# A decoder layer's MLP: the second matrix product done as seven block products instead of eight

## The chip, the cores and the metric

The kernel runs on one core of a Trainium2 chip as a single program. The metric is device time in microseconds (us). Three runs of the kernel before gave 1417.79, 1421.07 and 1423.99 us; the median, 1421.07 us, is the time to compare with. The execution that the profile shows is a fourth one.

## The reference, cut to what matters

One layer handles 1024 prompt tokens and 8 sample tokens together, so the activations have 1032 columns. The part that matters here is its end, the squared-ReLU MLP with 1024 channels and 4096 hidden units, and the final norm:

```python
hf = _rmsnorm(x, norm_ffn_g)
a = jax.nn.relu(jnp.einsum('btd,df->btf', hf, w_up))
x = x + jnp.einsum('btf,fd->btd', a * a, w_down)
...
y_prompt = _rmsnorm(xp, norm_final_g)
y_sample = _rmsnorm(xs, norm_final_g)
```

All numbers are float32. Ahead of the MLP stand a pooling mixer, gated linear attention and a cross-attention into 256 memory tokens.

## The kernel before

Activations lie transposed: 128 channels on the partitions, the 1032 tokens along the free dimension. TensorE multiplies in a rounded float32 format, so each operand is split into a high and a low part: ScalarE casts the value (`hi`, line 155), VectorE subtracts the cast from the value (`lo`, line 156), and a product is three matmuls, hi by hi, hi by lo and lo by hi. The helper `split` does that for weights and activations alike.

The MLP's way up (lines 1027 to 1160) already uses Winograd's form of Strassen's algorithm. `w_up` is cut into 2 by 2 quarters (halves of the input channels, halves of the hidden units), the activations into 2 by 2 quarters (halves of the channels, and tokens 0 to 511 against 512 to 1031), and seven products of sums of quarters, named "1" to "7", take the place of eight. A product of a 512-token block is one matmul of 512 columns per weight block and part; one of 520 tokens is two of 260 columns. `first_products` does products "1" and "2" for each of 16 blocks m of 128 hidden units and leaves quarter c11 in DRAM; `other_products` then does the other five for each m, adds them up on VectorE, applies ReLU and square on ScalarE (lines 1088, 1089) and writes the three quarters c22, c21 (`u3`) and c12 to the scratch tensor `hd` in DRAM from ScalarE's queue (line 1090).

The way down (lines 1163 to 1326) is a plain product. It walks over eight blocks `fb` of 512 hidden units: four tiles of hidden activations are loaded from `hd` and split (`block`), and for each of the 8 output chunks c of 128 channels a weight tile is loaded and split (`down_w`), 4 x 3 x 3 matmuls of 344 columns accumulate in PSUM (`gemm_steps`, line 192), and VectorE adds the result to the residual X (line 1207). The last block is walked in three column groups of 384, 384 and 264 tokens (line 1239) so that the final norm of finished tokens (`finish`) can run beside it; the last three token tiles are normed at the end.

All DMA transfers on the way down are issued by SyncE (SP), in its program order. The order in which instructions stand on each engine is made by the framework's scheduler from the code's order and the pools. Tiles come from pools with a fixed number of buffers: `S` has 19 large slots; `tmp` has 4 (line 68); `wp` holds raw and split weights (line 67); `mp` and `accp` are PSUM.

Of the kernel before, what the change touches and what calls it, by code (L numbers as in the profile page):

```python
# [8 lines left out]
F32 = mybir.dt.float32  # L9
# [7 lines left out]
P = 128  # L17
D = 1024
# [42 lines left out]
def body(ctx, tc, a, o):  # L61
# [968 lines left out]
    hd = dr.tile([2 * MU, P, NT], F32, name="hd")  # L1030
# [56 lines left out]
    def hidden_out(c, half, t):  # L1087
        A.activation(out=t, in_=t, func=AF.Relu)
        A.activation(out=t, in_=t, func=AF.Square)
        A.dma_start(hd[c][:, TH[half]], t)  # L1090

    def first_products(m):
# [8 lines left out]
        hidden_out(m, 0, c11)  # L1101

    def other_products(m):
# [36 lines left out]
        hidden_out(MU + m, 1, c22)  # L1140
        hidden_out(MU + m, 0, u3[:, :HA])
        hidden_out(m, 1, c12)
# [20 lines left out]
    X = []  # L1163
    for i in range(4):
        t = slot([P, 2, NT], F32, "x%d" % i)
        SY.dma_start(t, xd[2 * i:2 * i + 2].rearrange("c p n -> p c n"))
        X.append(t)

    gfin = slot([P, 2, 512], F32, "gfin")
    SY.dma_start(gfin.rearrange("p x n -> p (x n)"), a["norm_final_g"].unsqueeze(0).broadcast_to([P, D]))  # L1170
    WD = []

    w_down = a["w_down"][0].rearrange("(i k p) c -> p i k c", i=2, p=P)

    def down_raw(fb, c, name):

        raw = wp.tile([P, FC, P], F32, tag="raw", name=name, bufs=3)
        for i in range(2):
            SY.dma_start(raw[:, 2 * i:2 * i + 2, :], w_down[:, i, 2 * fb:2 * fb + 2, c * P:(c + 1) * P])
        return raw  # L1180

    def down_w(fb, c):
        return w_split(down_raw(fb, c, "wdn"))

    def block(fb, k):

        t = T("hid")
        SY.dma_start(t, hd[(k // 2) * MU + 2 * fb + k % 2])
        b_ = slot([P, 2, NT], F32R, "b")
        split(b_[:, 0, :], b_[:, 1, :], t)  # L1190
        return two(b_)

    def last_w(c):

        wd = slot([P, 2, 2, FC, P], F32R, "wd")
        for i in range(2):
            raw = down_raw(FB - 1, c + i, "wdl")
            split(wd[:, i, 0], wd[:, i, 1], raw)
            WD.append(wd[:, i])

    B = [block(0, k) for k in range(FC)]
    for fb in range(FB - 1):
        nxt = []
        for c in range(KC):
            acc = gemm_chunk(down_w(fb, c), B, "wdn")
            xc = X[c // 2][:, c % 2, :]
            V.tensor_tensor(out=g3(xc), in0=acc, in1=g3(xc), op=ALU.add)  # L1207
            if c % 2:
                nxt.append(block(fb + 1, c // 2))
                if fb == FB - 2:  # L1210
                    last_w(c - 1)
        B = nxt


    def turn_out(pt, t, c):

        n = min(P, NT - t * P)
        PE.transpose(pt[:n, (c % 4) * P:(c % 4 + 1) * P], X[c // 2][:, c % 2, t * P:t * P + n], ident)

    def rows(t):  # L1220
        return o["y_p"][0, t * P:(t + 1) * P, :].rearrange("p (x n) -> p x n", x=2)

    def finish(t):
        pt = accp.tile([P, NG, 512], F32, tag="acc", name="pty")
        for c in range(KC):
            turn_out(pt[:, c // 4], t, c)
        y = T("y", D).rearrange("p (x n) -> p x n", x=2)
        sc = sm.tile([P, 4], F32, tag="fin", name="sc")
        A.activation(out=y, in_=pt[:, :2], func=AF.Square, accum_out=sc[:, 0:1])
        V.tensor_scalar(out=sc[:, 1:2], in0=sc[:, 0:1], scalar1=1.0 / D, scalar2=EPS, op0=ALU.mult, op1=ALU.add)  # L1230
        rsqrt_(sc[:, 2:3], sc[:, 1:2], sc[:, 3:4])
        V.scalar_tensor_tensor(out=y, in0=pt[:, :2], scalar=sc[:, 2:3], in1=gfin, op0=ALU.mult, op1=ALU.mult)
        SY.dma_start(rows(t), y)

    def down(c, t0, ks, acc):
        q0, q1 = t0 * P, min((t0 + 3) * P, NT)
        for k in ks:
            for i, (x, y) in enumerate(((0, 0), (0, 1), (1, 0))):
                PE.matmul(acc[:, :q1 - q0], WD[c][:, x, k, :], B[k][y][:, q0:q1],  # L1239
                          start=(k == 0 and i == 0), stop=(k == FC - 1 and i == 2))  # L1240
        if ks[-1] == FC - 1:
            xc = X[c // 2][:, c % 2, q0:q1]
            V.tensor_tensor(out=xc, in0=acc[:, :q1 - q0], in1=xc, op=ALU.add)

    def acc_l():
        return mp.tile([P, 512], F32, tag="m", name="accl")


    wide = accp.tile([P, NG, 512], F32, tag="acc", name="accw")
    acc = [acc_l(), acc_l(), wide[:, 0], wide[:, 1]]  # L1250
    for ks in (range(FC - 1), range(FC - 1, FC)):
        for c in range(4):
            down(c, 0, ks, acc[c])
    for c in range(4, KC):
        down(c, 0, range(FC), acc_l())

    for c in range(KC):
        down(c, 3, range(FC), acc_l())
        if c < 3:
            finish(c)  # L1260
# [95 lines left out]
```

## Time and profile before

| | us |
|---|---|
| median of three runs | 1421.07 |
| profiled execution, its own time | 1412.17 |
| span of the profile | 1410.2 |
| TensorE busy | 1365.6 (97% of the span) |
| VectorE busy | 816.6 (58%) |
| ScalarE busy | 538.3 (38%) |
| GpSimd busy | 170.7 (12%) |

The profile lists for each engine the instructions with their times, and for an idle time what ended it. A busy TensorE is a modelled figure, since matmuls overlap; the distance between starts of successive matmuls is the better price of one. "DMA share" is the mean busy share of the core's 16 DMA engines; it can read slightly above 1.

### The profile page before, as it was taken

The page shows a single profiled execution, that of the slowest core. Times are in us where ns is not written, and L with a number is a line of the kernel's source. Part 1 is how long each engine was busy: PE and PEld are TensorE (multiplying, and loading weights), DVE is VectorE, ACT ScalarE, POOL GpSimd, SP SyncE. Part 2 cuts the span into 40 slices and gives each one's busy share as a digit, 9 for nine tenths or more (in the row PEclk, how much of TensorE's full clock was granted, in tenths as well). Part 3 has the DMA queues.
Part 4 walks back from the last instruction along what each step waited for, and adds up shares of the span by engine and source line. Part 5 has one row for each costly group of instructions (what it writes and reads, how often), then busy time and mean ns, then how long its engine had stood idle before and what let it go on. Part 6 is the DMA issues. An engine that isn't in the chain of part 4 may idle for free.

```text
span 1410.2 us, 22499 instructions
## 1 busy us (share of the span) xinstructions
PE 1365.6 (97%) x8830; PEld 1295.3 (92%) x8830; DVE 816.6 (58%) x1314; ACT 538.3 (38%) x1045; POOL 170.7 (12%) x143
## 2 busy tenths in 40 slices
PE   6999999999999899899999999999999999999997
PEld 6999999989999798778976899999999999999996
DVE  5775545785555767844694666666475433434434
ACT  5512112554344434444474454545462211112113
POOL 2143100431042204331200000000000000000000
PEclk9999999999999999999999999999999999999999
DMA  7711111384574455664459854442384313212102
GB/s 258 241 44 53 38 53 46 92 248 150 166 226 123 142 159 156 209 218 137 141 159 311 235 170 147 154 145 104 121 272 149 112 48 104 76 46 74 54 30 91
DMA packets 212146, 193.98 MB, mean 138 GB/s; under 512 B 11816, under 2 KB 180658, under 8 KB 211913
## 3 DMA queue, kind: packets, MB, share of 16 engines
q1 hardware_dynamic: 199369, 167.22, 38.8%
q10 hardware_dynamic: 12672, 25.34, 5.0%
q8 instruction: 69, 1.13, 0.3%
q14 instruction: 36, 0.29, 0.1%
HBM read 144.58 MB, written 47.94 MB: 137 GB/s over the span
## 4 chain that ended last, share of the span: by engine, by line
PE 83%; DVE 7%; DMA 4%; ACT 3%; issue 2%; SPq 1%; POOL 0%; DVEq 0%; ACTq 0%; POOLq 0%
PE acc L192 51%; PE acc L1084 21%; PE accl L1239 2%; DVE kt L834 2%; DMA kt<-in_cache_mem_k 1%; PE accv L708 1%; PE acck L341 1%; PE accsc L932 1%; DMA w<-in_w_up 1%; PE accpv L955 1%; DMA qb<-qdr 1%; PE psv L889 1%; PE accg L657 1%; PE accg L637 0%; ACT junk L314 0%
## 5 line engine op out<-in xcount | busy, mean ns | idle before, releaser
L1084 PE MATMUL acc<-T,wuph 128*128 128x260 f32 (+1 forms) x1408 | 286.8, 315 | 5.4 <-ACT p L1097 3.7
L192 PE MATMUL acc<-b,wuph 128*128 128x344 f32 x1344 | 248.8, 320 | 0.8 <-ACT b L155 0.7
L1084 PEld LDWEIGHTS acc<-T,wuph 128*128 128x128 f32 x1408 | 211.8, 189 | 26.2 <-ACT p L1097 7.6
L192 PEld LDWEIGHTS acc<-b,wuph 128*128 128x128 f32 x1344 | 218.7, 188 | 1.4 <-ACT b L155 1.0
L1084 PE MATMUL acc<-T,wupl 128*128 128x260 f32 (+1 forms) x704 | 178.8, 315 | 0.3 <-DVE wupl L156 0.3
L1207 DVE TENSOR_TENSOR x<-acc,x 128x1032 f32<-128x1032 f32 x56 | 69.0, 1231 | 147.1 <-PE acc L192 147.1
L192 PE MATMUL acc<-b,wupl 128*128 128x344 f32 x672 | 141.4, 319 | 0.0
L1084 PEld LDWEIGHTS acc<-T,wupl 128*128 128x128 f32 x704 | 115.3, 189 | 10.3 <-DVE wupl L156 1.9
L192 PEld LDWEIGHTS acc<-b,wupl 128*128 128x128 f32 x672 | 112.8, 188 | 0.0
L155 ACT CAST wuph<-wdn 128x512 fp32r<-128x512 f32 x56 | 34.8, 622 | 186.6 <-PE acc L192 182.6
L192 PE MATMUL acc<-c,womh 128*128 128x260 f32 (+2 forms) x384 | 80.4, 320 | 0.0
L192 PE MATMUL acc<-hm,wqmh 128*128 128x344 f32 x384 | 74.4, 327 | 0.0
L155 ACT CAST wuph<-w 128x512 fp32r<-128x512 f32 x64 | 39.8, 622 | 88.3 <-PE acc L1084 88.3
L192 PEld LDWEIGHTS acc<-c,womh 128*128 128x128 f32 x384 | 59.4, 188 | 5.9 <-ACT womh L155 0.8
L192 PEld LDWEIGHTS acc<-hm,wqmh 128*128 128x128 f32 x384 | 62.9, 190 | 0.6
L156 POOL TENSOR_TENSOR vs<-vt,vs 128x512 fp32r<-128x512 f32 x32 | 47.3, 1511 | 92.5 <-ACT vs L155 90.8
L192 PE MATMUL acc<-c,woml 128*128 128x260 f32 (+2 forms) x192 | 49.6, 320 | 0.0
L156 DVE TENSOR_TENSOR b<-hid,b 128x1032 fp32r<-128x1032 f32 x32 | 39.3, 1230 | 11.2 <-ACT b L155 11.1
L156 DVE TENSOR_TENSOR wupl<-w,wuph 128x512 fp32r<-128x512 f32 x64 | 42.6, 685 | 4.4 <-ACT wuph L155 4.4
L1239 PE MATMUL accl<-b,wd 128*128 128x384 f32 (+1 forms) x264 | 44.4, 321 | 0.0
L834 DVE SCALAR_TENSOR_TENSOR kt<-kt,qb 128x256 f32<-128x256 f32 x64 | 37.4, 640 | 7.4 <-DMA kt<-in_cache_mem_k 4.0
L1239 PEld LDWEIGHTS accl<-b,wd 128*128 128x128 f32 x264 | 41.5, 188 | 0.1
(394 smaller groups left out, 2513.2 us busy)
## 6 DMA issues: line engine op xcount, KB each, us to landing
hid<-hd SPq DMA_DIRECT2D x32, 516.0 KB
w<-in_w_up SPq DMA_DIRECT2D x64, 256.0 KB
wdn<-in_w_down SPq DMA_DIRECT2D x112, 128.0 KB
hd<-c ACTq DMA_DIRECT2D x32, 260.0 KB
x<-xd SPq DMA_DIRECT2D x16, 516.0 KB
xd<-x SPq DMA_DIRECT2D x16, 516.0 KB
vt<-in_cache_mem_v SPq DMA_DIRECT2D x16, 512.0 KB
kt<-in_cache_mem_k SPq DMA_DIRECT2D x32, 256.0 KB
```

The costliest lines, as they stand in the source:

```text
L155: A.copy(out=dst_hi, in_=src)
L156: (eng or V).tensor_tensor(out=dst_lo, in0=src, in1=f(dst_hi), op=ALU.subtract)
L192: PE.matmul(acc[:, g, :c1 - c0], w, X[k][j][:, c0:c1], start=(k == 0 and i == 0), stop=(k == len(W) - 1 and i == 2))
L341: PE.matmul(acc[:, 0, :MT], w[:, x, k, :], mn[y][:, k, :], start=(k == 0 and q == 0), stop=(k == KC - 1 and q == 2))
L657: PE.matmul(pso[:, 2 * p:2 * p + 2, :], qd[:, p, cs], stz[:, p], start=True, stop=False, skip_group_check=True)
L708: PE.matmul(acc[:, m, :], mn[x][:, k0 + kk, m * P:(m + 1) * P], y[:, kk, :], start=(k0 == 0 and kk == 0 and q == 0 and m == 0), stop=(k0 = ...
L834: V.scalar_tensor_tensor(out=kt[:, b, m, :], in0=kt[:, b, m, :], scalar=1.0, in1=qb[:, b, :], op0=ALU.mult, op1=ALU.mult, accum_out=ssc[:, ...
L889: PE.matmul(psv[:2 * NB, 0, :], pz[h % 2][:, bb + b, m, :], vs[:, j, b, m, :], start=(bb + b + m + j == 0), stop=(bb + b + m + j == NB + M ...
L932: PE.matmul(av[:, i, :], Q[2 * h + kk][x][:, ts_], KV[h][:, y, 0, kk, :], start=(i % 2 == 0 and n == 0), stop=(i % 2 == 1 and n == 5), ski ...
L1084: PE.matmul(acc, w, t[k // 2][:, k % 2, j, c0:c1], start=(first and k == 0 and i == 0), stop=(k == HK - 1 and i == 2), skip_group_check=True)
L1207: V.tensor_tensor(out=g3(xc), in0=acc, in1=g3(xc), op=ALU.add)
L1239: PE.matmul(acc[:, :q1 - q0], WD[c][:, x, k, :], B[k][y][:, q0:q1], start=(k == 0 and i == 0), stop=(k == FC - 1 and i == 2))
```

## The change

`w_down` is cut into quarters too, (output half i, hidden half j), and the way down becomes seven products "2", "1", "6", "3", "5", "4", "7", in that order. Each takes one factor made of sums of hidden quarters and one made of sums of weight quarters.

The factors of the hidden activations are made at the end of `other_products` and left in DRAM, one tensor `fd` for each product. Plain sums of two quarters are made in DRAM: ScalarE's queue stores one quarter, and a second transfer, issued by GpSimd with `accum_op=add`, adds the other quarter onto it. Differences ("3" and "4") are made by VectorE and stored by SP.

The weights are read quarter by quarter for each product. Where a factor is a sum (products "2", "1" and "5") SP loads the first quarter's block and a GpSimd transfer adds the second onto it in SBUF. Where it is a difference ("6" and "7") SP loads both and VectorE subtracts. A step is one half q of the 16 hidden blocks for one output chunk m: a weight tile of 512 KB, 24 matmuls of 512 columns or 48 of 260. Seven products x 4 chunks x 2 halves make 56 steps. After each step one of the next product's eight factor tiles is loaded and split; after each chunk VectorE adds the product's result to the quarters of X that it belongs to.

The pools `wp`, `tmp`, `sm`, `mp` and `accp` are closed after the way up and opened again in another layout (raw weight tiles 4 KB per partition instead of 2, four of them; `accp` 3 x 2 banks), where a new tile waits for the old tiles that it overlaps. The final norm of tokens 512 to 1031 runs in product "4", that of tokens 0 to 511 at the end, in product "7", whose last two chunks go in column groups of 256; two token tiles instead of three remain for the very end.

```diff
+    fd = {n: dr.tile([MU, P, HA if n in "247" else HB], F32, name="fd" + n) for n in "1234567"}
...
-    def hidden_out(c, half, t):
+    def relu2(t):
         A.activation(out=t, in_=t, func=AF.Relu)
         A.activation(out=t, in_=t, func=AF.Square)
-        A.dma_start(hd[c][:, TH[half]], t)
+    def add_out(n, m, x, y):
+        A.dma_start(fd[n][m], x)
+        G.dma_start(fd[n][m], y, accum_op=ALU.add)
...
-        hidden_out(MU + m, 1, c22)
-        hidden_out(MU + m, 0, u3[:, :HA])
-        hidden_out(m, 1, c12)
+        w = w4.rearrange("p a k n -> p (a k n)")
+        b11, b12, b21, b22 = p1, c12, u3[:, :HA], c22
+        SY.dma_start(b11[:, :HA], fd["2"][m])
+        relu2(b22)
+        A.dma_start(fd["5"][m], b22)
+        relu2(b21)
+        add_out("7", m, b21, b22[:, :HA])
+        add_out("1", m, b22, b11)
+        f4, f3 = w[:, :HA], w[:, HB:2 * HB]
+        V.tensor_tensor(out=f4, in0=b21, in1=b11[:, :HA], op=ALU.subtract)
+        SY.dma_start(fd["4"][m], f4)
+        relu2(b12)
+        add_out("6", m, b12, b11)
+        V.tensor_tensor(out=f3, in0=b12, in1=b22, op=ALU.subtract)
+        SY.dma_start(fd["3"][m], f3)
...
+    front.close()
+    wp = ctx.enter_context(tc.tile_pool(name="wpd", bufs=2, reuse_waits="tile"))
+    tmp = ctx.enter_context(tc.tile_pool(name="tmpd", bufs=4, reuse_waits="tile"))
...
+    DOWN = [("2", [(1, 0), (1, 1)], ALU.add, [(1, 0, ALU.add), (1, 1, ALU.subtract)]),
+            ("1", [(0, 0), (1, 1)], ALU.add, [(0, 0, ALU.add), (1, 1, ALU.add)]),
+            ("6", [(1, 0), (0, 0)], ALU.subtract, [(1, 1, ALU.add)]),
+            ("3", [(0, 0)], None, [(0, 1, ALU.add), (1, 1, ALU.add)]),
+            ("5", [(0, 0), (0, 1)], ALU.add, [(0, 0, ALU.subtract), (0, 1, ALU.add)]),
+            ("4", [(1, 1)], None, [(0, 0, ALU.add), (1, 0, ALU.add)]),
+            ("7", [(0, 1), (1, 1)], ALU.subtract, [(0, 0, ALU.add)])]
+    def factor(n, j):
+        w = width(n)
+        t = T("fac", 2 * w).rearrange("p (k n) -> p k n", k=2)
+        SY.dma_start(t, fd[n][2 * j:2 * j + 2].rearrange("k p n -> p k n"))
+        ff = slot([P, 2, 2, w], F32R, "F" + n)
+        split(ff[:, 0], ff[:, 1], t)
+        F.setdefault(n, []).append(ff)
+    def down_w(blocks, op, m, q, keep=False):
+        raw = []
+        for i, j in blocks:
+            src = w_down[:, j, q * UK:(q + 1) * UK, (i * MD_ + m) * P:(i * MD_ + m + 1) * P]
+            if raw and op == ALU.add:
+                G.dma_start(raw[0], src, accum_op=op)
+                continue
+            raw.append(wp.tile([P, UK, P], F32, tag="raw", name="wdn", bufs=4))
+            SY.dma_start(raw[-1], src)
+        if len(raw) > 1:
+            V.tensor_tensor(out=raw[0], in0=raw[0], in1=raw[1], op=op)
...
+        split(hi, lo, raw[0])
+        return hi, lo
+    def down_part(to, n, W, q):
+        for k in range(UK):
+            ff = F[n][(q * UK + k) // 2]
+            for i, (x, y) in enumerate(((0, 0), (0, 1), (1, 0))):
+                for acc, c0, c1 in to:
+                    PE.matmul(acc, W[x][:, k, :], ff[:, y, k % 2, c0:c1], start=(q == 0 and k == 0 and i == 0),
+                              stop=(q == 1 and k == UK - 1 and i == 2))
...
+    for j in range(MU // 2):
+        factor("2", j)
+    for i, j in ((1, 0), (1, 1), (0, 0), (0, 1)):
+        X[i, j] = slot([P, MD_, HB], F32, "x%d%d" % (i, j))
+        n = HA if j == 0 else HB
+        SY.dma_start(X[i, j][:, :, :n], xd[i * MD_:(i + 1) * MD_].rearrange("c p n -> p c n")[:, :, TH[j]])
...
+    for d, (n, blocks, op, outs) in enumerate(DOWN[:-1]):
+        nxt = DOWN[d + 1][0]
+        todo = list(range(MU // 2))
+        for m in range(MD_):
+            acc, to = down_acc(n)
+            for q in range(2):
+                down_part(to, n, down_w(blocks, op, m, q), q)
+                factor(nxt, todo.pop(0))
+            down_add(acc, outs, m)
```

How the change moves SP's queue at the border between the way up and the way down. Before, in the kernel's last stretch of the way up (`c_...<-p1d` are the loads of the last hidden blocks, `wdn` weights and `hid` hidden tiles of the way down):

```order
L1170 DMA gfin<-in_norm_final_g 128x1024
L1111 DMA c_9631<-p1d 128x512
L1111 DMA c_9791<-p1d 128x512
L1179 DMA wdn<-in_w_down 128x2x128 x2
L1111 DMA c_9951<-p1d 128x512
L1179 DMA wdn<-in_w_down 128x2x128 x2
L1111 DMA c_10111<-p1d 128x512
L1179 DMA wdn<-in_w_down 128x2x128 x2
L1188 DMA hid<-hd 128x1032 x2
L1179 DMA wdn<-in_w_down 128x2x128 x4
L1188 DMA hid<-hd 128x1032 x5
```

Now, with what each waits for in brackets (`fd_4134` is the tensor of factor "3", `fd_4133` of "2", `fd_4132` of "1"; `fac` a factor tile, `x_...` the quarters of X; the first row is the very last store of the way up):

```order
L1163 DMA fd_4134<-w_10247 128x520 [waits DMAHW5_49,DVE_49]
L1215 DMA fac<-fd_4133 128x2x512 [waits DMASW6_49,DMAHW1_49,DMASW4_49,DMAHW4_49,DMASW3_49,DMAHW6_49,Activation_49,Pool_49]
...
L1215 DMA fac<-fd_4133 128x2x512 [waits DMAHW6_49,DMAHW2_49,DVE_49]
...
L1215 DMA fac<-fd_4133 128x2x512 [waits DMAHW5_49,DMAHW1_49,DVE_49]
L1229 DMA wdn<-in_w_down 128x8x128
L1215 DMA fac<-fd_4132 128x2x520 [waits DMAHW2_49,DVE_49]
L1298 DMA x_10476<-xd 128x4x512 [waits PE_49]
L1298 DMA x_10479<-xd 128x4x520 [waits PE_49]
...
L1229 DMA wdn<-in_w_down 128x8x128 [waits DMAHW4_49,PE_49]
```

X, weights and hidden tiles of the way down stood among the loads of the way up; now all of them, with all eight factor tiles, stand behind its last store, the first weight tile behind the eighth factor tile, the second behind X.

GpSimd's queue before, to its end (memsets of a pad in the way up, then nothing on the way down):

```order
L1110 MEMSET c_9471 128x8
L1110 MEMSET c_9631 128x8
L1110 MEMSET c_9791 128x8
L1110 MEMSET c_9951 128x8
L1110 MEMSET c_10111 128x8
L1343 UNCONDITIONAL_BRANCH
```

And now (`fd_4138` and `fd_4137` belong to factors "7" and "6"; the rows of L1097 and L1226 are the adding transfers):

```order
L1118 MEMSET c_10252 128x8
L1097 DMA fd_4132<-c_10083 128x520
L1097 DMA fd_4138<-c_10086 128x512
L1097 DMA fd_4137<-c_10083 128x520
...
L1300 MEMSET x_10476 128x4x8
L1226 DMA wdn<-in_w_down 128x8x128
L1300 MEMSET x_10481 128x4x8
L1226 DMA wdn<-in_w_down 128x8x128 x23
```

GpSimd gets three adding transfers for each of the 16 blocks of the way up and 24 on the way down, each waiting in turn for the load or store that it adds to.

## Rows read from the trace of the kernel before

**Rows 1.** The page: busy time by engine, and the chain of waits by engine and line.
```profile
PE 1365.6 (97%) x8830; PEld 1295.3 (92%) x8830; DVE 816.6 (58%) x1314; ACT 538.3 (38%) x1045; POOL 170.7 (12%) x143
PE 83%; DVE 7%; DMA 4%; ACT 3%; issue 2%; SPq 1%; POOL 0%; DVEq 0%; ACTq 0%; POOLq 0%
```

**Rows 2.** Engine time by stretch; last columns: granted clock, DMA share, GB/s.
```profile
795.00:1025.00 230.00, 229.98 (x1731) 221.01 (x1731) 141.77 (x217) 112.17 (x193) 1.58 (x15) 1.00 0.47 151
1126.00:1171.00 45.00, 45.00 (x287) 45.00 (x286) 18.97 (x21) 9.00 (x12) 0.00 (x0) 1.00 0.31 94
```

**Rows 3.** The chain in order of time: start, us, what, count.
```profile
795.08 228.28 PE acc L1084 x1714
...
1028.81 4.62 DMA hid<-hd
...
1035.83 309.81 PE acc L192 x1962
...
1364.54 0.87 PE pty L1218 x8
...
1400.38 1.55 ACT junk L1286 x8
```

**Rows 4.** First and last start of the way down's matmuls, by line.
```profile
L192 PE MATMUL acc<-b,wuph x1344: 313/319/428, 1026.1 to 1344.8; 128*128 128x344 f32 x192
L192 PE MATMUL acc<-b,wupl x672: 313/318/324, 1027.1 to 1345.3; 128*128 128x344 f32 x168
L1239 PE MATMUL accl<-b,wd x264: 278/336/419, 1345.5 to 1399.3; 128*128 128x384 f32 x84, 128*128 128x264 f32 x48
```

**Rows 5.** TensorE's timeline in the way up: matmuls of 512 and 260 columns.
```profile
797.61 0.63 PE L1084 MATMUL acc<-T,wuph 128*128 128x512 f32 x2
798.07 0.39 PE L1084 MATMUL acc<-T,wupl 128*128 128x512 f32 x1
...
800.39 0.52 PE L1084 MATMUL acc<-T,wuph 128*128 128x260 f32 x3
...
806.00 0.64 PE L1084 MATMUL acc<-T,wuph 128*128 128x260 f32 x4
...
811.04 0.64 PE L1084 MATMUL acc<-T,wuph 128*128 128x260 f32 x4
```

**Rows 6.** End of block m = 14 of the way up: TensorE, VectorE, ScalarE.
```profile
1011.53 0.41 PE L1084 MATMUL acc<-T,wupl 128*128 128x260 f32 x2
...
1011.98 0.70 DVE L1139 TENSOR_TENSOR c<-acc,c 128x520 f32<-128x520 f32 x1 [0.25 <-PE acc L1084]
...
1014.16 0.64 ACT L1089 ACTIVATE c<-c 128x520 f32<-128x520 f32 x1
```

**Rows 7.** The hidden tiles' instructions: issue, cast, subtraction (min/median/max ns).
```profile
L1188 SPq DMA_DIRECT2D hid<-hd x32: 319/339/534, 1017.1 to 1208.9; - x32
L155 ACT CAST b<-hid x32: 1039/1057/1062, 1023.7 to 1311.6; 128x1032 fp32r<-128x1032 f32 x32
L156 DVE TENSOR_TENSOR b<-hid,b x32: 1223/1232/1236, 1025.2 to 1313.5; 128x1032 fp32r<-128x1032 f32 x32
```

**Rows 8.** Stretches with busy DMA engines, and two with TensorE waiting and restarting.
```profile
12.00:18.00 6.00, 4.84 (x22) 4.27 (x22) 2.48 (x9) 5.39 (x14) 1.17 (x1) 0.72 1.04 401
741.00:752.00 11.00, 10.73 (x47) 8.30 (x46) 8.91 (x15) 8.05 (x14) 0.00 (x0) 1.00 1.13 314
752.00:759.80 7.80, 5.01 (x20) 3.14 (x18) 2.93 (x5) 2.87 (x6) 0.00 (x0) 1.00 1.14 316
759.80:762.80 3.00, 2.96 (x7) 2.40 (x8) 0.00 (x0) 0.52 (x1) 0.00 (x0) 0.50 1.10 299
1038.00:1042.00 4.00, 4.00 (x27) 4.00 (x27) 4.00 (x5) 2.91 (x4) 0.00 (x0) 1.00 1.01 355
```

**Rows 9.** GpSimd: its work beside the way up, and its nearest larger instruction.
```profile
L1110 POOL MEMSET c<- 128x8 f32 x15 | 1.6, 105 | 211.3 <-DMA hd<-c 84.9 <-ACT wuph L155 83.0 <-PE acc L1084 15.6
L156 POOL TENSOR_TENSOR vs<-vt,vs 128x512 fp32r<-128x512 f32 x32 | 47.3, 1511 | 92.5 <-ACT vs L155 90.8 <-issue 1.7
```

More of the change, by code (lines that the diff above doesn't have):

```diff
@@ L1160, in body @@
         other_products(m)
[L1163 to L1199, printed above, removed]
@@ L1231, in finish @@
         rsqrt_(sc[:, 2:3], sc[:, 1:2], sc[:, 3:4])
-        V.scalar_tensor_tensor(out=y, in0=pt[:, :2], scalar=sc[:, 2:3], in1=gfin, op0=ALU.mult, op1=ALU.mult)
+        V.scalar_tensor_tensor(out=y, in0=pt[:n], scalar=sc[:, 2:3], in1=gfin[:n], op0=ALU.mult, op1=ALU.mult)
         SY.dma_start(rows(t), y)
[L1235 to L1260, printed above, removed]
-    sc = sm.tile([P, 4, 3], F32, tag="fin3", name="sc", bufs=1)
@@ new lines, in body, with last_part @@
+    n, blocks, op, outs = DOWN[-1]
+    for m in range(2):
+        acc, to = down_acc(n)
+        for q in range(2):
+            down_part(to, n, down_w(blocks, op, m, q), q)
+        down_add(acc, outs, m)
+    W = {(m, q): down_w(blocks, op, m, q, True) for m in (2, 3) for q in range(2)}
+    sc = sm.tile([P, 4, 3], F32, tag="fin3", name="sc3", bufs=1)
+    ys = [T("yl", D) for _ in range(2)]
+    junk = T("junk", D)
+    def last_part(g, m):
+        acc = mp.tile([P, 512], F32, tag="m", name="accl")[:, :HA // 2]
+        c0 = g * HA // 2
+        for q in range(2):
+            down_part([(acc, c0, c0 + HA // 2)], n, W[m, q], q)
+        x = X[0, 0][:, m, c0:c0 + HA // 2]
+        V.tensor_tensor(out=x, in0=x, in1=acc, op=ALU.add)
@@ new lines, in last_sum @@
+    def last_sum(i, cs, p):
+        x = cs.start // 512
+        gs = slice(cs.start % 512, cs.start % 512 + cs.stop - cs.start)
+        for t in range(2):
+            A.activation(out=junk[:, cs], in_=p[t], func=AF.Square, accum_out=sc[:, i, t:t + 1])
+        if i:
+            V.tensor_tensor(out=sc[:, 0, :2], in0=sc[:, 0, :2], in1=sc[:, i, :2], op=ALU.add)
+        for t in range(2):
+            V.tensor_tensor(out=ys[t][:, cs], in0=p[t], in1=gfin[:, x, gs], op=ALU.mult)
+    for m in (2, 3):
+        last_part(0, m)
@@ new lines, in body @@
+    last = [accp.tile([P, 2, 512], F32, tag="acc", name="ptl") for _ in range(2)]
+    for t in range(2):
+        for c in (4, 5, 6, 7, 0, 1):
+            turn_out(last[t][:, c // 4, c % 4 * P:c % 4 * P + P], 2 + t, c)
+    last_sum(0, slice(512, 1024), [last[t][:, 1] for t in range(2)])
+    last_part(1, 2)
+    for t in range(2):
+        finish(t)
+    last_part(1, 3)
+    for t in range(2):
+        turn_out(last[t][:, 0, 2 * P:3 * P], 2 + t, 2)
+    last_sum(1, slice(0, 3 * P), [last[t][:, 0, :3 * P] for t in range(2)])
@@ new lines, in body @@
+    end = mp.tile([P, 4, P], F32, tag="m", name="ptend")
+    for t in range(2):
+        turn_out(end[:, t, :], 2 + t, 3)
+    last_sum(2, slice(3 * P, 4 * P), [end[:, t, :] for t in range(2)])
+    V.tensor_scalar(out=sc[:, 1, :2], in0=sc[:, 0, :2], scalar1=1.0 / D, scalar2=EPS, op0=ALU.mult, op1=ALU.add)
+    rsqrt_(sc[:, 2, :2], sc[:, 1, :2], sc[:, 3, :2])
+    for t in range(2):
+        for x in range(2):
+            y = ys[t][:, x * 512:(x + 1) * 512]
+            r = sc[:, 2, t:t + 1]
+            if (t, x) == (0, 1):
+                A.activation(out=y, in_=y, func=AF.Copy, scale=r)
+            else:
+                V.tensor_scalar(out=y, in0=y, scalar1=r, scalar2=None, op0=ALU.mult)
+            SY.dma_start(rows(2 + t)[:, x], y)
```

143 lines of the change are left out of this document (60 added, 83 removed).

## The prediction

> **What bounds the kernel now.** I read the page first: TensorE is busy 97% of the span and holds 83% of the chain of waits; VectorE has 58%, ScalarE 38%, GpSimd 12% [rows 1]. Then the stretches. In the way up from 795 to 1025 us TensorE is busy 229.98 of 230 us at the full granted clock, VectorE 62%, ScalarE 49%, GpSimd nearly nothing; the DMA engines have a share of 0.47. On the way down TensorE is busy 45.00 of 45 us, VectorE 42%, ScalarE 20%, DMA share 0.31 [rows 2]. Then the chain in order of time: 1962 matmuls of the way down follow each other for 309.81 us with nothing between [rows 3]. So the end is set by how many columns TensorE streams, and any time in which it has nothing to stream is lost. Last I looked for what the DMA engines can do, since the change gives them much more: their share reaches 1 at 401 GB/s with 4 KB rows, at 314 GB/s with the 512-byte rows of the weights, at 355 GB/s with a mixture [rows 8].
>
> **TensorE's work.** Before, one matmul of 344 columns costs 309.81 / 1962 = 0.158 us [rows 3]. The whole way down runs from 1026.1 to about 1399.6 us, 373.5 us [rows 4]. In it are 72 transposes at 0.87 / 8 us each [rows 3], 7.8 us, and about 1.3 us of waiting at its start (1962 of 2016 matmuls are in the unbroken run, the other 54 are worth 8.5 us and take 9.8). Matmuls alone: 364.4 us.
>
> After, a product is 4 chunks x 16 blocks x 3 parts: 192 matmuls of 512 columns ("2", "4", "7") or 384 of 260 ("1", "6", "3", "5"). The way up does these shapes already: 12 matmuls of 512 columns between 797.61 and 800.39 us, 0.232 us each; 42 of 260 columns between 806.00 and 811.04 us (seven times four and two), 0.120 us [rows 5]. So 576 x 0.232 + 1536 x 0.120 = 133.6 + 184.3 = 317.9 us; the transposes stay 72. TensorE saves 364.4 - 317.9 = 46.5 us. A step is 24 x 0.232 = 5.6 or 48 x 0.120 = 5.8 us.
>
> **The border between the two ways.** Before, hidden tiles and weights of the way down are loaded ahead and TensorE goes straight on. Now the eight factor tiles, X and the first weights all stand in SP's queue behind the store of the last factor "3". With E as the end of the last matmul of the way up:
>
> - In block 14 TensorE's product ends at 1011.8, VectorE's addition follows at 1011.98 and the last ReLU square ends at 1014.80 [rows 6], so E + 3.0. VectorE's difference (0.70) and two issues on SP at 0.34 [rows 7]: the first factor tile leaves at E + 4.4.
> - A hidden tile of 516 KB took 4.62 us to land in like traffic [rows 3]: E + 9.0. Tiles two to four, 0.53 MB each at 355 GB/s, land by E + 13.5. `tmp` has four buffers, so tile five leaves only when tile one is split, and tile eight when tile four is: cast 1.06 and subtraction 1.23 [rows 7], E + 15.8. The first weight block stands behind it: E + 16.2, landing 4.6 later at E + 20.8.
> - GpSimd then adds the second quarter onto it. The trace has no adding transfer. From below it is a load like others (4.6 us with its landing), from above twice that, as it reads both operands. I take 4.6, the only row of such a landing: E + 25.4. Cast of the weights 1.06: TensorE starts at E + 26.5. Minus the 1.3 us of before: **+25.2 us** (19 if landings take 3 us, 31 with the double price).
> - The second weight block stands behind another factor tile and the 4.2 MB of X. 4.8 MB at 355 to 401 GB/s are 12 to 13 us after E + 20.8, its own load 1.7, the adding 4.6, the cast 1.1: about E + 41, while step one ended at E + 32. **+9 us** (3 to 14).
>
> Two restarts of TensorE: after the wait at 759.8 us the granted clock was 0.50 for 3 us, the lower of the two levels, then full again [rows 8]: 1.5 us each, **+3 us**.
>
> **The rest.** Steps of the three sum products move 0.52 MB twice in 512-byte rows and a factor tile: 1.05 / 0.314 + 0.53 / 0.401 = 4.7 us of DMA, against 5.6 to 5.8 us of TensorE. They hide while an adding transfer costs one load, but there is little slack and the queue starts full: **+2 us** (0 to 13, rival two). Product "6" loads two blocks a step with buffers for two steps: **+1 us** (0 to 8). VectorE per step: two or three passes of 1.23 us and half of two additions of 0.70 [rows 6, 7], 3.2 to 4.4 us, hidden under 5.8; ScalarE's two casts, 2.1 us, as well.
>
> In the way up each block gains two VectorE passes (1.4 us; 62% becomes 71%), and traffic. Per block: weights 1.05 MB at 314 GB/s, 3.3 us; two small loads 0.52 MB at 355, 1.5; six stores 1.58 MB at 401, 3.9; three adding transfers of 0.26 MB, doubled, at 355, 4.4. That is 13.1 us of a block of 12 x 0.232 + 96 x 0.120 = 14.3 us; the chain's 1714 matmuls in 228.28 us agree [rows 3]. Loads of the next weights run many blocks ahead, and the adding transfers have the whole next block to land, so: **+1 us** (0 to 13, rival three). The very end norms two token tiles instead of three; ScalarE's last squares were 1.55 us [rows 3]: **-1 us**. GpSimd did 0.1 us of memset per block there [rows 9], so its queue is free for the transfers.
>
> Sum: -46.5 + 25.2 + 9 + 3 + 2 + 1 + 1 - 1 = -6.3 us. The profiled execution took 1412.17 us; the median of the runs is 1421.07, 0.6% above. I put the difference on the median: 1414.8 us.
>
> **Rivals.**
>
> One, GpSimd is the pace (slower). Place: the 24 adding transfers of weights in "2", "1" and "5"; each has 1024 pieces of 512 bytes, and they go one after the other through GpSimd. Nothing in the trace prices it: an issue on SP is 0.34 us [rows 7]; GpSimd itself takes 1.51 us to work through 128x512 elements [rows 9], a tile is two of these, 3.0 us. Both are below a step, which speaks against it. Each 1 us over the mean step of 5.7 costs 24 us. It decides the sign from (6.3 + 7.1) / 24 = 0.56 us over, 6.3 us per transfer; at 7.4 us the time is 1455, at 9 us 1494.
>
> The Trainium skill (SBUF — State Buffer, section "SBUF: two separate sides") says that a transfer issued by GpSimd has its descriptors written by GpSimd's cores, and that VectorE in a two-port mode locks these out: 620 ns alone, about 3100 ns beside a copy. No run here shows it. By it 2.5 us would be added to a transfer, an estimate, which a step still covers; the sum would change at the border alone, by two times 2.5 us.
>
> Two, an adding transfer costs the DMA engines a second read. The pace of the sum steps is then 1.57 / 0.314 + 0.53 / 0.401 = 6.3 us, 0.5 to 0.7 over TensorE's, for the 14 steps after the border, 9 us; the border grows by 4 to 6 us. In all -6.3 - 2 + 9 + 5 = +6: 1427 us. For it: the addition needs both operands. Against: no row. Product "5" escapes, since "3" ahead of it has one block per step and fills four buffers.
>
> The skill's page Collectives: The Full Stack ("Stop ④") describes an addition inside a DMA engine as two reads and one write with the addition free. That is this rival's mechanism; no run here shows it so far.
>
> Three, the way up falls behind its transfers. 13.1 of 14.3 us hides; with the adding transfers at three passes a block takes 3.3 + 1.5 + 3.9 + 6.7 = 15.4 us, 1.1 too many, for the nine blocks that also load weights: 10 in place of 1, 1424 us. For it: the share was above 1 with TensorE waiting at 741 to 760 us [rows 8]. Against: 0.47 now [rows 2].
>
> **How the numbers follow.** My own case 0.60, between 1397 (all low ends: -46.5 + 19 + 3 + 1.5 - 1) and 1432 (31, 14, 3, 3, 4, 3, -1). Rival one 0.20, two 0.12, three 0.08. About 0.5%, 7.1 us, is what can be told from no change. My case lies at that border: 0.39 faster, 0.18 same, 0.03 slower. Two gives 0.07 same and 0.05 slower, three 0.01, 0.03 and 0.04, one 0.20 slower. Sums: faster 0.40, same 0.28, slower 0.32. The range goes from 1397 to 1455, which leaves out the worse half of rival one.
>
> **What would show it.** TensorE's matmuls on the way down should number 576 (96 of them split in two) and 1536 at 0.23 and 0.12 us apart. The gap between the last L1087 and the first L1247 matmul should be about 26 us, with a second one of about 9 us a step later whose releaser is an adding transfer. From product "6" on TensorE should stand still little. I am wrong if waits for adding transfers run all through "2", "1" and "5" (rival one if the DMA share is low there, two if it is near 1), if the way up from 795 us on takes over 235 us, or if the border is closed in under 15 us, which would give some 1400 us.

## The result and the profile after

The changed kernel takes **1464.73 us** (median of 4 runs, 1464.52 to 1466.82), the kernel before 1420.75 us beside it; the ratio is **1.031, 95% interval 1.030 to 1.033**. The forecast was 1414.8 us, its range ended at 1455. The change is slower by 44 us, and the forecast was wrong in sign and size.

The page of the changed kernel (busy time, the queues, the chain), which answers to [rows 1]:

```profile
span 1463.0 us, 22667 instructions
...
PE 1337.6 (91%) x8734; PEld 1240.7 (85%) x8734; DVE 862.5 (59%) x1350; ACT 579.9 (40%) x1060; POOL 249.9 (17%) x217
...
q1 hardware_dynamic: 257993, 213.56, 47.9%
q0 software_dynamic: 31872, 25.30, 12.7%
...
HBM read 195.04 MB, written 73.37 MB: 183 GB/s over the span
...
PE 67%; DMA 16%; DVE 9%; ACT 3%; issue 3%; SPq 2%; POOL 0%; ACTq 0%; DVEq 0%; POOLq 0%
```

The chain was 83% TensorE and is 67%; 16% of it is now transfers. The new line among the queues (packets, MB, share of 16 engines) is `q0`, GpSimd's. In it 25.30 MB cost 12.7% of sixteen engines' span: 25.30 MB / (0.127 x 16 x 1463.0 us) = 8.5 GB/s on an engine, 136 GB/s on all. SP's `q1` moves 213.56 MB for 47.9%, 305 GB/s on all.

Where the time went, by TensorE's instructions. First and last start of the matmuls of either way:

```profile
L1087 PE MATMUL acc<-T,wupl x704: 278/284/629, 701.0 to 1051.3; 128*128 128x260 f32 x128, 128*128 128x512 f32 x48
...
L1247 PE MATMUL accd<-F,wdnh x1344: 277/283/796, 1094.6 to 1422.5; 128*128 128x260 f32 x146, 128*128 128x512 f32 x46
```

The part of the way up that took 230.9 us (795.08 to 1026.0, [rows 3, 4]) goes from 799.27 to 1051.6, 252.3 us. The gap between the ways is 43.0 us. The way down runs from 1094.6 to 1449.8, 355.2 us, in place of 373.5. What follows takes 13.2 us in place of 10.6. So the difference of the two spans, 1463.0 - 1410.2 = 52.8 us, is: start 4.2, way up 21.4, border 43.0, way down -18.3, end 2.6 (0.1 is rounding). The start is not the change's: in the runs below the same stretch began anywhere between 793 and 805 us. The spans differ by more than the 44 us of the medians because the profiled execution before was itself 8.6 us faster than its median; that of the changed kernel lies on its median.

The border in the timeline of the changed kernel (start, duration, engine, line; in brackets the wait before it):

```profile
1055.95 15.64 SPq L1215 DMA_DIRECT2D fac<-fd  x8
...
1062.03 1.04 ACT L157 CAST F<-fac 128x1024 fp32r<-128x1024 f32 x1 [7.45 <-DMA fac<-fd]
...
1071.64 0.46 SPq L1229 DMA_DIRECT2D wdn<-in_w_down  x1
...
1072.96 5.94 SPq L1298 DMA_DIRECT2D x<-xd  x4
...
1078.73 1.60 POOL L1226 DMA_DIRECT2D wdn<-in_w_down  x1 [20.53 <-DMA wdn<-in_w_down]
...
1093.47 1.04 ACT L157 CAST wdnh<-wdn 128x1024 fp32r<-128x1024 f32 x1 [15.99 <-DMA wdn<-in_w_down]
...
1094.57 1.22 PE L1247 MATMUL accd<-F,wdnh 128*128 128x512 f32 x2 [42.95 <-ACT wdnh L157]
```

With E = 1051.6: first factor tile issued at E + 4.3 (forecast 4.4), landed at 10.4 (9.0); weights issued at 20.0 (16.2) and landed just before GpSimd's issue of the adding transfer at 27.1 (20.8); that one landed at 41.8, 14.7 us after its issue in place of 4.6. The gap of 43.0 us stands against the forecast's 26.5 (25.2 after taking off the 1.3 us of before). Of these 16.5 us, 10.1 are that one landing. That X stands in front of it is not the reason: with the same X in front and no addition (e4 below) the landing took 8.3 us, and with X loaded a quarter at a time (x1 below) it still took 13.4, in a gap of 41.5.

Each line of adding transfers, and what waits for them (weights, then activations; landing is min/median/max):

```profile
L1226 POOL DMA_DIRECT2D wdn<-in_w_down x24: 1549/1549/1598, 1078.7 to 1329.5; - x24
...
  ACT wdnh L157: 83.3, 14
...
DMA to landing us min/median/max: 6.2/12.3/18.6
```
```profile
L1097 POOL DMA_DIRECT2D fd<-c x48: 856/930/1564, 820.1 to 1057.2; - x48
...
DMA to landing us min/median/max: 4.2/5.8/9.2
```

GpSimd is done with a transfer of weights after 1.55 us; the landing is what takes 12. The 83.3 us are 14 waits of ScalarE's casts, over all three products. Two stretches of the changed kernel, the blocks of the way up that still load weights and the first steps of the way down (columns: stretch, its length, busy us of TensorE, of its weight loads, of VectorE, ScalarE and GpSimd; then granted clock, DMA share, GB/s):

```profile
820.00:940.00 120.00, 105.40 (x776) 100.28 (x774) 70.28 (x111) 49.80 (x86) 19.40 (x28) 0.99 0.88 232
```
```profile
1095.00:1195.00 100.00, 86.88 (x473) 73.98 (x473) 41.47 (x41) 29.01 (x29) 23.31 (x15) 0.91 1.24 255
```

TensorE stands for 14.6 of 120 and 13.1 of 100 us, with the DMA engines at a share of 0.88 and 1.24, but at 232 and 255 GB/s. Before, a share near 1 gave 299 to 401 GB/s [rows 8]: the engines are as busy and move less.

The chain in order of time (start, us, what):

```profile
1090.17 8.39 DMA wdn<-in_w_down
...
1099.10 13.44 DMA wdn<-in_w_down
...
1127.62 18.60 DMA wdn<-in_w_down
...
1164.04 14.41 DMA wdn<-in_w_down
...
1224.84 138.64 PE accd L1247 x1100
```

Loads, adding transfers and factor tiles take turns up to 1225 us; from the second of the four chunks of "6" on, through "3" and "5", TensorE runs without a break: "3" needs one block per step, and "5" finds its buffers filled ahead.

### The profile page after: what moved, and what is told of

The parts are those of the page before. It is cut to its first block, busy times and chain, and to the rows that moved or that the text cites. A ratio compares the mean times of both kernels' runs of the same rounds, so it can differ in the third digit from the quotient of the medians.

```text
span 1463.0 us, 22667 instructions
## 1 busy us (share of the span) xinstructions
PE 1337.6 (91%) x8734; PEld 1240.7 (85%) x8734; DVE 862.5 (59%) x1350; ACT 579.9 (40%) x1060; POOL 249.9 (17%) x217
## 3 DMA queue, kind: packets, MB, share of 16 engines
q1 hardware_dynamic: 257993, 213.56, 47.9%
q0 software_dynamic: 31872, 25.30, 12.7%
HBM read 195.04 MB, written 73.37 MB: 183 GB/s over the span
## 4 chain that ended last, share of the span: by engine, by line
PE 67%; DMA 16%; DVE 9%; ACT 3%; issue 3%; SPq 2%; POOL 0%; ACTq 0%; DVEq 0%; POOLq 0%
PE acc L194 28%; PE acc L1087 15%; PE accd L1247 13%; DMA wdn<-in_w_down 5%; DMA fac<-fd 3%; DMA fd<-c 3%; DVE kt L836 2%; DMA kt<-in_cache_mem_k 1%; PE acck L343 1%; PE accl L1247 1%; PE accv L710 1%; PE accsc L934 1%; DMA fd<-w 1%; DMA wup<-in_w_up 1%; DMA c<-p1d 1%
## 5 line engine op out<-in xcount | busy, mean ns | idle before, releaser
L1247 PE MATMUL accd<-F,wdnh 128*128 128x260 f32 (+1 forms) x1344 | 270.2, 314 | 53.2 <-ACT wdnh L157 53.2
L1247 PEld LDWEIGHTS accd<-F,wdnh 128*128 128x128 f32 x1344 | 203.9, 192 | 68.6 <-ACT wdnh L157 54.9
L1087 PE MATMUL acc<-T,wupl 128*128 128x260 f32 (+1 forms) x704 | 181.0, 318 | 16.5 <-DVE wupl L158 16.5
L1247 PE MATMUL accd<-F,wdnl 128*128 128x260 f32 (+1 forms) x672 | 169.8, 315 | 7.4 <-DVE wdnl L158 7.2
L1247 PEld LDWEIGHTS accd<-F,wdnl 128*128 128x128 f32 x672 | 111.2, 192 | 17.9 <-DVE wdnl L158 10.9
L157 ACT CAST wdnh<-wdn 128x1024 fp32r<-128x1024 f32 x52 | 54.5, 1049 | 170.9 <-PE accd L1247 87.1
L158 DVE TENSOR_TENSOR wdnl<-wdn,wdnh 128x1024 fp32r<-128x1024 f32 x52 | 63.5, 1221 | 75.4 <-ACT wdnh L157 75.4
L158 DVE TENSOR_TENSOR F<-fac,F 128x1040 fp32r<-128x1040 f32 (+1 forms) x56 | 68.3, 1231 | 33.2 <-ACT F L157 32.4
L157 ACT CAST F<-fac 128x1040 fp32r<-128x1040 f32 (+1 forms) x56 | 58.6, 1055 | 59.7 <-DMA fac<-fd 51.2
L1226 POOL DMA_DIRECT2D wdn<-in_w_down x24 | 37.3, 1555 | 235.4 <-DMA wdn<-in_w_down 199.0
L1097 POOL DMA_DIRECT2D fd<-c x48 | 42.2, 1046 | 149.3 <-DMA fd<-c 129.6
L158 POOL TENSOR_TENSOR vs<-vt,vs 128x512 fp32r<-128x512 f32 x32 | 46.5, 1485 | 98.7 <-ACT vs L157 98.7
## 6 DMA issues: line engine op xcount, KB each, us to landing
wdn<-in_w_down POOLq DMA_DIRECT2D x24, 512.0 KB, 12.3
```

Source lines behind the costliest of these rows:

```text
L157: A.copy(out=dst_hi, in_=src)
L158: (eng or V).tensor_tensor(out=dst_lo, in0=src, in1=f(dst_hi), op=ALU.subtract)
L1087: PE.matmul(acc, w, t[k // 2][:, k % 2, j, c0:c1], start=(first and k == 0 and i == 0), stop=(k == HK - 1 and i == 2), skip_group_check=True)
L1097: G.dma_start(fd[n][m], y, accum_op=ALU.add)
L1226: G.dma_start(raw[0], src, accum_op=op)
L1247: PE.matmul(acc, W[x][:, k, :], ff[:, y, k % 2, c0:c1], start=(q == 0 and k == 0 and i == 0), stop=(q == 1 and k == UK - 1 and i == 2))
```

## The experiments

All ratios are to the kernel before, run beside them on the same chip; the short names (e1, x1) are those that the expectations use. The kernel before moves by some us from one set of runs to the next (1417 to 1421), so ratios are compared rather than times.

Theory A: an adding transfer costs the DMA engines far more than a plain one, in both ways. Rivals: B, the order of SP's queue at the border and the bytes; C, GpSimd's issues; D, VectorE.

**Weights' sums on VectorE (e1).** The edit takes the adding transfer out of `down_w`; the second quarter is loaded by SP and added as in "6":

```diff
-            if raw and op == ALU.add:
-                G.dma_start(raw[0], src, accum_op=op)
-                continue
```

Expected: 

> Both quarters of the weights of products 2, 1 and 5 are loaded by SP and added by VectorE, as product 6 does already; the 24 adding transfers of weights are gone, the 48 of activations stay. Theory A (an adding transfer costs the DMA engines about twice a load and lands in 12 us in place of 5): the waits for wdnh and wdn in products 2 and 1 (29 us of stalls) shrink by half or more and the border by some 8 us: about 1440 us, with the way up unchanged. Theory B (the order of SP's queue at the border and the sheer bytes): the bytes are the same, so 1460 or more, the border still 40 us. Theory C (GpSimd's issue of 1.55 us each): small, 1458 to 1464.

Measured: 1439.24 us, 1.016 (1.013 to 1.020) of before, in place of 1.031: some 22 us less. The gap between the ways is 30.8 us in place of 43.0. A holds for this half; B and C do not. The edit also lets the two quarters load side by side instead of one after the other; e4 tells the two apart.

**Activations' sums on VectorE (e2).** The sums for "7", "1" and "6" are made in SBUF and stored once:

```diff
-        add_out("7", m, b21, b22[:, :HA])
-        add_out("1", m, b22, b11)
...
+        V.tensor_tensor(out=b21, in0=b21, in1=b22[:, :HA], op=ALU.add)
+        SY.dma_start(fd["7"][m], b21)
...
-        add_out("6", m, b12, b11)
...
+        V.tensor_tensor(out=f6, in0=b12, in1=b11, op=ALU.add)
+        SY.dma_start(fd["6"][m], f6)
+        V.tensor_tensor(out=b11, in0=b22, in1=b11, op=ALU.add)
+        SY.dma_start(fd["1"][m], b11)
```

Expected: 

> The sums for factors 7, 1 and 6 are made by VectorE in the way up and stored once; the 48 adding transfers of activations are gone, with 48 of the plain stores' seconds; the weights' adding transfers stay. Theory A: the way up takes back most of the 21 us that it lost, so about 1445 us, and the border a few us, since no adding transfer is in flight there. Theory B (the chain from the reload of factor 2 through SP's in-order queue sets the way up): the reload stays, so the way up stays at 245 us or more and the whole at 1458 or more. Theory D (VectorE, with three more passes a block, becomes late itself): 1465 or more, with waits of TensorE for wupl.

Measured: 1438.97 us, 1.016 (1.012 to 1.019). Its chain has the way up unbroken again, as in [rows 3]:

```profile
803.92 228.32 PE acc L1087 x1714
```

The reload of factor 2 stayed and cost nothing, and so did VectorE's three passes more per block.

**Both (e3).** Expected: 

> Both together: no adding transfer at all. Theory A: the two gains add, about 1420 us, that is within 1% of the kernel before; what remains of the border is the order of the queue (25 us). Theory B: 1450 or more.

Measured: 1419.59 us, 1.001 (0.999 to 1.003), the time of the kernel before. The two gains add: 0.0152 and 0.0155 of the ratio, 0.0301 together. What the algebra saves (46.5 us) is spent on the border, 28.1 us, and on stalls and lower clock in the first steps: the way down takes 344.0 us against 317.9 + 7.8 of work. The wait ahead of its first matmul:

```profile
1063.06 1.22 PE L1247 MATMUL accd<-F,wdnh 128*128 128x512 f32 x2 [28.07 <-ACT wdnh L157]
```

**Same transfers, no addition (e4).** `accum_op` is dropped at both places, the transfers stay on GpSimd between the same buffers; the sums are left out.

Expected: 

> The same 72 transfers from GpSimd between the same places, but without the addition: they overwrite (so the sums are left out, products 2, 1, 5, 7 and 6 use the second quarter alone). Theory A in its strict form (the addition's second read is what costs): nearly the time of e3 or better, 1415 to 1430 us, and packets of GpSimd's queue at 45 ns as SP's. Theory C (GpSimd's queue and its order, whatever is transferred): as after, 1460 or more, packets still at 90 ns.

Measured: 1422.43 us, 1.004 (1.002 to 1.006). GpSimd's queue and the landings on its page, the waits for its weights, and the border:

```profile
q0 software_dynamic: 7296, 25.30, 5.4%
...
wdn<-in_w_down POOLq DMA_DIRECT2D x24, 512.0 KB, 7.7
fd<-c POOLq DMA_DIRECT2D x32, 260.0 KB, 2.9
...
  ACT wdnh L157: 16.9, 3
...
1066.51 1.22 PE L1247 MATMUL accd<-F,wdnh 128*128 128x512 f32 x2 [35.55 <-ACT wdnh L157]
```

The same 25.30 MB take 5.4% of 1420.7 us in place of 12.7% of 1463.0, that is 330 GB/s in place of 136, a factor of 2.4. They also land in 7.7 and 2.9 us in place of 12.3 and 5.4. So the addition is worth some 40 of the 44 us (42.3 between the medians, 39 by the ratios), and C falls. By stages, changed kernel against this one: way up 252.3 and 231.2 us, border 43.0 and 35.6, way down 355.2 and 340.9. GpSimd's queue as such is worth some 4 us over the whole (1.004 against e3's 1.001, with intervals that overlap). At the border it costs 7.5: there the second quarter is fetched only when the first has landed, 35.55 us in place of e3's 28.07, and its landing took 8.3 us without any addition.

The plain transfers are also cut into larger pieces: there are a quarter as many packets, each longer, 168 ns and not 45. (The expectation was put on the wrong unit; bytes per engine time are the one to compare.) That the cut is not the price can be read from e1, where only the adding stores of activations are left, beside ScalarE's plain stores (`q10`) in packets of much the same size:

```profile
q0 software_dynamic: 6912, 12.72, 6.0%
q10 hardware_dynamic: 14976, 29.60, 5.7%
```

Over the span of 1437.7 us that is 147 GB/s in packets of 1.84 KB with the addition and 361 GB/s in packets of 1.98 KB without. For the weights, in 512-byte pieces, it is 126 GB/s with the addition (e2: 12.58 MB, 6.9% of 1443.6 us) against 314 without [rows 8].

**X later (x1).** In the changed kernel the quarters of X move behind the first four weight blocks.

```diff
...
                 down_part(to, n, down_w(blocks, op, m, q), q)
+                if late_x:
+                    load_x(*late_x.pop(0))
                 factor(nxt, todo.pop(0))
```

Expected: 

> The changed kernel with its adding transfers, and one thing moved: the four quarters of the stream X (4.2 MB) are no longer loaded ahead of the second weight block but one after each of the first four weight blocks. Theory A (the adding transfers set the pace in products 2 and 1): the bytes up to product 6 are the same, so what the second weight block gains the later ones lose: 1460 us, at most 5 us gained. Theory B (the order of the queue at the border): the second stall at 1095 to 1113 us goes, 10 us or more: 1450.

Measured: 1458.25 us, 1.030 (1.026 to 1.034): not to be told from the changed kernel's 1.031. Alone, the order gives nothing that can be told while the adding transfers are there. The second weight block's stall fell from 7.0 to 3.0 us, but stalls of 3.3 and 4.0 us follow, and over the first 100 us of the way down TensorE stands for 13.4 us in place of 13.1.

**X later, without adding transfers (x2).** Expected: 

> Without adding transfers (e3), and X late as in x1. In e3 the gap between the ways is still 31 us and some 18 us of stalls follow in products 2 and 1. If these come from the order of SP's queue, the second stall (12.65 us of chain for the second weight block) goes and the time falls by 5 to 12 us, to 1408 to 1415; if from the pace of the DMA engines, 1417 to 1422.

Measured: 1414.12 us, 0.998 (0.996 to 1.000), against 1.001 (0.999 to 1.003) without the move: some 5 us, at the edge of what the intervals tell apart.

**Factor 2 early as well (x3).** The tiles are split in place during the last eight blocks of the way up:

```diff
...
     for m in range(MU):
         other_products(m)
+        if m >= MU - 8:
+            factor2(m - (MU - 8))
...
```

Expected: 

> As x2, and the eight tiles of factor 2 are loaded and split during the last eight blocks of the way up, in place, so that at the border only the first weight block is waited for. The gap between the ways was put at 25 us in the prediction, 16 of them the factor tiles: it should shrink to 12 to 16 us, and the time to 1390 to 1400. If the way up becomes longer instead (TensorE waiting for wupl behind the eight extra splits), 1405 or more.

Measured: 1404.77 us, 0.991 (0.989 to 0.993), faster than before. The border, by the timeline of this kernel:

```profile
1047.48 1.22 PE L1257 MATMUL accd<-F,wdnh 128*128 128x512 f32 x2 [13.76 <-ACT wdnh L157]
```

The gap is 13.8 us, as expected, 14 less than in the kernel with no adding transfer (28.07; the 31 that x2's expectation read there were too much). The time fell less than the expected 1390 to 1400, since the way up became longer, 239.6 us in place of x2's 231.1. The early tiles hold slots, so that near its end TensorE waits for a block's own weights (4.16 us of the chain are `w<-in_w_up` at 1009 us); with six early tiles (x6) it takes 234.2.

**First weights early as well (x4).** Expected: 

> As x3, and the first two weight blocks are loaded in the last block of the way up, into slots that factors 4 and 6 of the way up leave. Then nothing is waited for at the border: a gap under 4 us and 1378 to 1390 us, faster than the kernel before by 2% or more. If the DMA engines are the bound of products 2 and 1 whatever the order, the stalls come later instead and the time stays at 1395 or more.

Measured: 1404.78 us, 0.991 (0.989 to 0.993). The gap shrank to 5.7 us, the time did not move:

```profile
1047.91 1.22 PE L1273 MATMUL accd<-F,wdnh 128*128 128x512 f32 x2 [5.66 <-ACT wdnh L157]
```

The gap was expected under 4 us; of the expectation's two times it is the second that came, 1395 us or more. The steps behind it still stand: over 1060 to 1180 us TensorE is idle for 8.5 of 120 us, at a share of 1.02 (columns as above):

```profile
1060.00:1180.00 120.00, 111.45 (x750) 101.28 (x749) 81.88 (x78) 42.02 (x41) 0.00 (x0) 0.99 1.02 300
```

**Product 3 second, six tiles early (x5).** Expected: 

> As x4, with three things to lighten products 2 and 1: product 3, which loads one weight block per step in place of two, comes second; the quarters of X are loaded when they are first needed; only six of the tiles of factor 2 are loaded early, so that the last two blocks of the way up keep the slots for their weights. If the bytes of the first 16 steps set what x4 still loses (some 20 us of stalls between 1048 and 1167 us), 1385 to 1395 us; if it is the latency of each step's chain of loads, additions and casts, 1400 to 1405.

Measured: 1401.16 us, 0.987 (0.981 to 0.993), the fastest of all, but its interval overlaps the two above. By the expectation's own alternatives this is the time for latency, not for the bytes of the first steps. The traces do not settle it: in 1060 to 1180 us TensorE now stands for 2.8 us in place of 8.5, yet the whole way down takes 344.3 us against x4's 343.2.

**The same without the early weights (x6).** Expected: 

> As x5, but the first two weight blocks are not loaded early (as in x3). x3 and x4 took the same time, so the early weights were worth nothing while the DMA engines were the bound afterwards; with the lighter steps behind them they should be worth the gap, 6 to 10 us: 1392 to 1404 us. If x6 equals x5, the gap is hidden behind another wait.

Measured: 1404.72 us, 0.988 (0.983 to 0.994), the same as x5 within the intervals. So the early weights have no value that these runs show, and whether the order of products has any stays open.

**Two plain transfers for one adding one (y1).** Each of the 72 is replaced by two plain ones; the sums are left out.

Expected: 

> As e4, but each of the 72 adding transfers is replaced by two plain ones of the same bytes, one after the other, from GpSimd to the same place (the sums are left out). After against e4 showed that the addition itself costs 42 us. If an addition is worth one more transfer of its bytes (rival two's second read), this kernel should take about the time of the changed kernel, 1455 to 1470 us. If it stays near e4, 1420 to 1435, an addition costs more than a second transfer, and the slower packets of GpSimd's queue (93 against 43 ns) and their landing are a price of their own.

Measured: 1495.41 us, 1.054 (1.049 to 1.059), a miss on both sides. The second of a pair goes to the same place, so it waits for the first to land (for the weights GpSimd stands 153.9 us in 23 such waits), and a buffer of weights is held for three landings in a row. A window of its way down shows another loss (columns as above), and its page what GpSimd's queue took:

```profile
1140.00:1220.00 80.00, 62.25 (x395) 57.25 (x394) 29.37 (x29) 20.56 (x22) 13.19 (x15) 0.87 0.72 217
...
q0 software_dynamic: 14592, 50.60, 10.3%
```

TensorE stands for 17.8 of 80 us with the DMA share at 0.72: latency, not occupancy (in the 60 us before, the share is 1.00). So the time of this run does not price an addition. It does say that a chain of landings through four buffers stalls at such a length even with the engines not full. The queue gives a price: 50.60 MB are again moved at 330 GB/s, 10.3% of 1490.8 us for the pairs of plain transfers against 12.7% of 1463.0 for the adding ones. One adding transfer costs the engines more than two plain ones in larger pieces.

**Adding transfers that nobody waits for (z1).** That left a question on the way up: is it the DMA time that the adding transfers take from others, or the waits for their landing? To the kernel without them, 42 of the same size are added whose result, source and target no one needs:

```diff
+        for i in (1, 2, 3):
+            if m >= i:
+                G.dma_start(p1d[m - i], f(TT["5"][0])[:, 0, 0, :HA], accum_op=ALU.add)
```

Expected: 

> As e3 (VectorE makes all sums), and 42 adding transfers of 0.26 MB are put beside it in the way up, from a tile that is not reused onto rows of p1d that nobody reads any more: no instruction needs them or their buffers. Theory A1 (what the adding transfers cost is the time of the DMA engines that they take from others): the way up is lengthened as in the changed kernel, 42/48 of the 20 us that e2 gave back, so 1434 to 1440 us. Theory A2 (the cost is that buffers, the reload of factor 2 and the plain store in front wait for a landing): nobody waits here, so the way up keeps its 228 us of unbroken matmuls and the time is 1415 to 1423.

Measured: 1431.55 us, 1.009 (1.006 to 1.012), some 11 us over the kernel without them (1.009 against 1.001), between the two expectations. The stretch 820 to 940 us, first without, then with these transfers, then in e1, where the activations' adding transfers are waited for:

```profile
820.00:940.00 120.00, 120.00 (x902) 115.25 (x902) 102.11 (x160) 59.41 (x104) 0.83 (x8) 1.00 0.65 212
```
```profile
820.00:940.00 120.00, 110.09 (x811) 103.52 (x810) 90.53 (x146) 50.11 (x88) 20.72 (x31) 1.00 0.95 251
```
```profile
820.00:940.00 120.00, 110.46 (x797) 105.01 (x796) 72.97 (x114) 53.37 (x92) 19.33 (x28) 0.97 0.89 235
```

The share goes from 0.65 to 0.95 and TensorE loses 9.9 us, against 9.5 in e1 and 14.6 in the changed kernel, whose way up has the same instructions as e1's. By the length of the way up it is 244.8 us against 231.2 without, 13.6 more, where e1 has 249.5, 18.3 more; 42 of 48 of that are 16. By the time it is some 11 of 17 us (42/48 x 19.7 us, from 1439.24 in e1 to 1419.59 in e3). So their occupancy alone makes two thirds of the loss or more. The rest may be the waits for landings; it was not measured apart.

## Why the prediction was wrong

**TensorE's work: right.** The 2208 matmuls of the way down are there (1344 + 672 + 192), and the unbroken run of 1100 is worth 1052 x 0.120 + 48 x 0.232 = 137.4 us against 138.64. The 46.5 us are saved; the way down is only 18.3 us shorter because 355.2 - 317.9 - 7.8 = 29.5 us of standing and of lower clock lie in it.

**An adding transfer as one load: the step that failed.** The text had the right place and two bounds ("from below a load like others, from above twice that", 4.6 and 9.2 us) and took the lower one, as the only row of such a landing. Measured: 12.3 us by the median, 14.7 for the first, above both bounds, and 2.4 times the engines' time of a plain transfer. Every term that the sum priced with it went with it. Border: a gap of 26.5 became 43.0. Not all of that is the addition: without it (e4) the gap is still 35.6. There the same transfer lands in 8.3 us and by the median in 7.7, so 4.6 was too little even for a plain transfer in this queue. Steps of "2" and "1": a step moves 0.52 MB plainly at 314 GB/s [rows 8], 0.52 MB adding at 136 and a factor tile at 401, 1.7 + 3.9 + 1.3 = 6.9 us, an estimate, against TensorE's 5.7; the text had 4.7 and "+2". Way up: three adding transfers of 0.26 MB are 5.7 us in place of 4.4, so a block's 13.1 us become 14.4 against 14.3. On average this only just fills a block and would cost a few us, an estimate; "+1" became +21, most of which these averages leave unexplained. That the way up loses it to the addition is shown (231.2 us again in e2, e3 and e4), and that most of it comes from occupancy (z1).

**Rivals two and three had the mechanism, at too low a price and one at a time.** Two (a second read) was put at 1427 us, three (the way up behind its transfers) at 1424. Both came, at 2.4 times a plain transfer, and added up. The sign named for them, waits for adding transfers through "2" and "1" with the DMA share near 1, is what the trace shows (83.3 us in 14 waits of ScalarE; share 1.24). The forecast treated them as exclusive cases, but both hang on one unknown price. The Trainium skill's page Collectives: The Full Stack (section "Stop ④") has the addition itself free between two reads and one write. That alone does not give this case's price: with and without the addition the profile counts the same 195.04 MB read, so no row shows the second read, and the engines take 2.4 times as long, where a second read at the price of a second transfer would make it 2.0. What inside the engine takes the time, no run here shows.

**Rival one fell.** 24 issues of 1.55 us (1.60 at most) are far below a step's 5.7. The Trainium skill (SBUF — State Buffer, section "SBUF: two separate sides") lets VectorE's two-port modes hold up the descriptors that GpSimd writes, 3100 ns in place of 620 in its example. The 24 issues here lie between 1549 and 1598 ns with VectorE at 41% beside them: no such delay shows. But VectorE's passes beside them add or subtract two tensors, and the example's is a copy, so this case does not test it.

**The second stall (+9) and the restarts: right in kind.** The second weight block waited behind factor and X as described, and TensorE stood 7.0 us for it; it is 8.0 in e4, so the addition is not needed for it. The granted clock was 0.67 over 1095 to 1115 us. But moving X away (x1) gave nothing measurable: the stall shrank to 3.0 us and later ones took its place.

**The very end: -1 became +2.6.** The chain there has `out_y_p<-y`, 5.04 us, in front of the next tile's square: the output buffer is waited for. It is there without any addition too (e4: 5.05 us) and absent in e3 and x2, whose end takes 11.5 us. So it is not the addition's; what decides on it was not tried apart.

## What to carry to other kernels

A transfer that adds is not a transfer with a free addition: before an engine with slack (VectorE was busy 41%) is spared a pass of 0.7 to 1.2 us, price the DMA engines' time, not the bytes. Where one unknown price stands in several terms of a sum, its two ends move all of them at once, and the range must be made with all terms at the same end. Read the DMA share together with GB/s: busy engines at a low rate (1.24 at 255 GB/s) were the sign of expensive transfers here, a share well under 1 with a standing TensorE (0.72) that of landings in series.

## What the runs showed of the hardware

- Adding transfers: 136 GB/s over sixteen engines (q0, 25.30 MB); 140 in the last experiment (11.01 MB, 5.5% of 1426.8 us), all of it SBUF to DRAM in whole rows. The same transfers without the addition: 330 GB/s, in a quarter as many packets; plain stores of ScalarE in packets like those of e1's adding stores: 361 against 147.
- GpSimd's own time for an issue was longer with the addition, and with the smaller packets that came with it: 1.55 us against 0.88 for 512 KB of weights (24 issues each).
- With the DMA engines full (share 1.16 over 1082 to 1091 us), an issue on SP became long itself: 7.80 us for one factor tile, against a median of 0.42 for all 56. What stood behind it in SP's queue waited with it. That the full engines are the cause was not tried apart.
